# Attention scores on 64 rows of TensorE, two heads in turn, and begun ahead of the value projection

## The chip, the cores and the metric

One core of one Trainium2 chip runs the whole program in one launch. The metric is the device time in microseconds (us), the median over timed runs of the same program on the same chip; lower is better. The profile is of one more execution, and its own time stands beside its span below.

## What is computed

The reference is a decoder trunk of two layers on 256 tokens of width 1024, in float32. Layer 0 mixes tokens with a gated recurrence, layer 1 with sparse attention; each is followed by an MLP with squared ReLU. The change lies in layer 1, the attention. There are 16 query heads of 64 columns in 4 groups of 4, and each group has keys and values of its own in three branches: compressed (15 blocks), selected and sliding window. With 256 tokens, at most 4 blocks to select from and a window of 512, the selected and the window branch both see all earlier tokens; they differ in keys and values. Cut to what matters here:

```python
s_c = jnp.einsum('qghd,ngd->ghqn', qf, kc) - slopes * d_c      # compressed keys
s_s = jnp.einsum('qghd,gqkd->ghqk', qf, k_sel) - slopes * d_s  # selected keys
s_w = jnp.einsum('qghd,kgd->ghqk', qf, kw) - slopes * d_w      # window keys
p_c, p_s, p_w = (_masked_softmax(s, m) for s, m in ((s_c, m_c), (s_s, m_s), (s_w, m_w)))
o = g[..., 0:1] * (p_c @ v_c) + g[..., 1:2] * (p_s @ v_s) + g[..., 2:3] * (p_w @ v_w)
```

## The kernel before

**Split numbers.** Large products are done with numbers split in two: hi is the float32 value rounded to the float32r type, lo is what the rounding left. A product of weights and activations is three matmuls that add up in one PSUM bank (`mm3`, lines 317 to 320): hi x hi, hi x lo, lo x hi. A weight piece (128 x 1024 numbers, 512 KB) is loaded by SP into one of five raw buffers, split by ACT or DVE into `whi` (a cast), and by DVE into `wlo` (a subtraction, `diff`, line 323).

**The planner.** In the attention section nothing is issued directly. Each step is put to a `Plan` with its engine, an estimated duration, what it reads and writes, and a due time `t`. `Plan.emit` makes a list schedule from that and improves it in a few rounds; the order in which each engine issues is the order of the plan's start times. The constants at the top (`TSTAGE`, `FPS`, `SEEDS`) shift due times and choose among plans.

**The attention section** (from line 828) does the following. `cproj` makes the inputs of the compressed branch, `hidden` (L955) and `kc_out` (L965), `vc_out` (L984) its keys and values. `kchunk` projects keys of two groups at once, so that 128 partitions hold 2 groups x 64 columns, and `qchunk` projects queries of two heads at once in the same way. `values` (L1005 to L1007) projects values and gates in four pieces. Then for each of 16 heads `scores` (L1098, L1099) multiplies queries with keys, DVE (L1109, L1116) adds the distances and takes the largest while it copies the rows out of PSUM, ACT (L1112) takes the exponential, `rescale` divides by the sums, `transposes` (L1147) turns the rows, and `pv` (L1162) multiplies with the values, each matmul of it writing 64 of 128 partitions (one head of two). `compressed` (L1072 its transpose) does the compressed branch for four heads. Projections of the later queries and keys and of the output (`out_t`) are laid between as fillers.

**How one score product uses 128 rows.** A head has only 64 columns, and hi and lo of the queries are packed into the two halves of the 128 partitions. For a head in the lower half, the query tile `sa` holds hi in both halves at first, and then its other half is overwritten with lo by a DMA inside the chip (`move`, issued by SP); `sb` does the same for the head in the upper half. The keys `kh` hold hi twice, in both halves (again by a `move`), so that one matmul gives hi x hi + hi x lo; `kl` holds lo in the head's own half and zeros, set by a memset on POOL, in the other, so that a second matmul adds lo x hi:

```python
e.matmul(view(z()), x[:, qs], keys_(kh), start=True, stop=False)   # L1098
e.matmul(view(z()), x[:, qs], keys_(kl), start=False, stop=True)   # L1099
```

Three such parts make a head: the first 128 queries against 128 keys of both branches and the compressed ones (288 columns), the second 128 against 256 keys of one branch and the compressed ones (272), and against 256 of the other (256). Each part takes one of three banks (`sbank`), which is free again when DVE has read it.

Of the kernel before, what the change touches and what calls it, by code (L numbers as in the profile page):

```python
# [19 lines left out]
P = 128  # L20
# [11 lines left out]
NPT, NTL = 3, 3  # L32
TSTAGE, FPS = 5.0, 3.25
CST = (3.5, 7.5, 11.5, 15.2)
SEEDS, ROUNDS, SHIFT = (64, 5), 6, 1.5
# [16 lines left out]
def weight_pieces():  # L52

    order = []
    order += [{"c": ("in", 8 + i), "y": ("in", i)}[k] for k, i in RG_ORDER if k != "g"]
    order += [("out", m) for m in range(8)]
    order += mlp_pieces(0)
    order += [("ck", 0), ("ck", 1), ("cv", 0), ("cv", 1), ("ks", 0), ("kw", 0)]
    order += [("v", i) for i in range(4)]
    order += [("q", m) for m in range(4)]  # L60
    order += [("ks", 1), ("kw", 1)]
    order += [("q", m) for m in range(4, 8)]
    order += [("o0", m) for m in range(4)]
    order += [("o1", m) for m in range(4)]
    order += mlp_pieces(1)
    return order
# [153 lines left out]
def trunk_kernel(ctx: ExitStack, tc: tile.TileContext, x_in, vec_in, const_in, w2_in, wts, out):  # L220
# [607 lines left out]
    with ExitStack() as ph:  # L828
# [12 lines left out]
        tt, tl = many([P, S], F32, "tt", 3), many([P, S], F32R, "tl", NTL)  # L841
# [4 lines left out]
        kh, kl = (at.tile([P, 4 * GK + NCP], F32R, name=n) for n in ("kh", "kl"))  # L846
        kpair = lambda y, g, n: y[:, g * GK:g * GK + 2 * (S + NCP)].rearrange("p (b k) -> p b k", b=2)[:, :, :n]
        kcomp = lambda y: y[:, :4 * GK].rearrange("p (g k) -> p g k", g=4)[:, :, P:PC]
# [20 lines left out]
        add("pool", 1.74, lambda e: e.memset(kl.bitcast(F32), 0.0), w=["kl"], t=-9)  # L869
# [3 lines left out]
        def turn():  # L873
            ti["n"] += 1
            n = ti["n"]
            return tt[n % 3], ("tt", n % 3), tl[n % NTL], ("tl", n % NTL)
# [6 lines left out]
        def qchunk(c, b, t, step):  # L883
            z, zk = proj_t("q", c, b, t, step)
            t += 4 * step
            x, xk, l_, lk = turn()
            a, b_ = sa[c % NQ], sb[c % NQ]
            ak, bk = ("sa", c % NQ), ("sb", c % NQ)
            add("dve", 0.4, lambda e: e.scalar_tensor_tensor(x, z(), cst[:, C_QS + c:C_QS + c + 1], rs,
                                                             op0=OP.mult, op1=OP.mult), r=[zk, "rs"], w=[xk], t=t)  # L890
            add(HI, copy(a, x), r=[xk], w=[ak, ak + (1,)], t=t + 0.5)
            add(HI, copy(b_, x), r=[xk], w=[bk, bk + (1,)], t=t + 0.5)
            add("dve", 0.34, diff(l_, x, a), r=[xk, ak, ak + (1,)], w=[lk], t=t + 1)
            move(a[64:], l_[:64], [lk], [ak + (1,)], t + 1.2)
            move(b_[:64], l_[64:], [lk], [bk + (1,)], t + 1.2)

        def kchunk(gp, br, b, t, step):
            z, zk = proj_t(("ks", "kw")[br], gp, b, t, step)
            t += 4 * step
            x, xk, l_, lk = turn()  # L900
            add("dve", 0.34, lambda e: e.tensor_tensor(x, z(), rs, op=OP.mult), r=[zk, "rs"], w=[xk], t=t)
            x, l_ = two_blocks(x), two_blocks(l_)
            for hf in range(2):
                g = gp * 2 + hf
                add(HI, copy(kset(kh, g, br), x), r=[xk], w=[("k", g, br), ("k", g, br, 1)], t=t + 0.5)
            add("dve", 0.34, diff(l_, x, kset(kh, gp * 2, br)), r=[xk, ("k", gp * 2, br), ("k", gp * 2, br, 1)], w=[lk], t=t + 1)
            for hf in range(2):
# [4 lines left out]
        def kkeys(g, br):  # L912
            return [("k", g, br), ("k", g, br, 1), ("k", g, br, 2)]
# [20 lines left out]
        def cproj(i, gp, b, t, step):  # L934
            z, zk = proj_t(("ck", "cv")[i], gp, b, t, step)
            t += 4 * step
            x, xk, _, _ = turn()
# [25 lines left out]
        def kc_out(t):  # L963
# [4 lines left out]
            add("act", 0.1, lambda e: e.copy(kcomp(kh), o4()), r=[("ps", 6)], w=["kch"], t=t)  # L968
            for hf in range(2):
                own = own_(hf)  # L970
                add("dve", 0.15, lambda e, own=own, hf=hf: e.tensor_tensor(
                    kcomp(kl)[own, hf::2], o4()[own, hf::2], kcomp(kh)[own, hf::2].bitcast(F32), op=OP.subtract),
                    r=[("ps", 6), "kch", "kl"], w=[("kcl", hf)], t=t)
# [17 lines left out]
        def values(t):  # L991
            banks = ((2, 3), (4, 5))
            ncol = (S + 48, S)
            vz = [[zview(("v", h, b), banks[h][b], lambda x, b=b: x[:, :ncol[b]]) for b in range(2)] for h in range(2)]
            for i in range(4):
                wh, wl, wk = weight("v", i, t + 2.8 * i)
                for kk in range(2):
                    k = 2 * i + kk
                    for h in range(2):
                        def run(e, wh=wh, wl=wl, k=k, kk=kk, h=h):  # L1000
# [8 lines left out]
                            t=t + 2.8 * i + 1.4 * kk + 0.7 * h)  # L1009
            t += 11.2  # L1010
# [64 lines left out]
        def scores(s, t):  # L1075
            p, c, hf = heads[s]
            g = 2 * p + hf
            slope = float(2.0 ** (-8.0 * (g * 4 + c + 1) / 16))
            cc = (4 * p + c) % NQ
            x, xk = (sb, sa)[1 - hf][cc], ("sb" if hf else "sa", cc)  # L1080
            xk = [xk, xk + (1,)]
            mx, sm, pt = mxs[s % 4], sms[s % 4], pts[s % NPT]
            a, cj = s // 4, s % 4
            cview = lambda y, n, k: y[:, :2 * n].rearrange("p (b k) -> p b k", b=2)[:, :, :k]
            parts = ((0, lambda x: cview(x, PC, PC), lambda y: kpair(y, g, PC), (0, 1), 0.26),
                     (1, lambda x: x[:, :S + NCP], lambda y: y[:, g * GK:g * GK + S + NCP], (0,), 0.25),
                     (1, lambda x: x[:, :S], lambda y: y[:, g * GK + S + NCP:(g + 1) * GK], (1,), 0.23))
            for i, (qc, view, keys_, sets, d) in enumerate(parts):
                nk = (qc + 1) * P
                n = sn["n"]  # L1090
                sn["n"] += 1
                b = sbank[n % 3]
                bk = [("ps", b)]
                z = zview(("s", s, i), b, lambda x: x)

                def run(e, z=z, qc=qc, view=view, keys_=keys_):
                    qs = slice(qc * P, (qc + 1) * P)
                    e.matmul(view(z()), x[:, qs], keys_(kh), start=True, stop=False)  # L1098
                    e.matmul(view(z()), x[:, qs], keys_(kl), start=False, stop=True)  # L1099
                add("pe", d, run, r=xk + ["kl", "kch", ("kcl", 0), ("kcl", 1)] + kkeys(g, 0) + kkeys(g, 1), w=bk, t=t)  # L1100
                for b in sets:
                    o, j = qc * 2 * P + b * nk, 2 * qc + b
                    mk, pk = ("mx", s % 4, j), ("pt", s % NPT, qc, b)
                    row = pt[:, o:o + nk]
                    dist = cst[:, C_D0 + qc * P:C_D0 + qc * P + nk]
                    src = (lambda z, b=b: cview(z(), PC, P)[:, b]) if qc == 0 else (
                        (lambda z: z()[:, :S]) if b else lambda z: cview(z(), PC, P))
                    shape = two_blocks if (qc, b) == (1, 0) else lambda y: y
                    add("dve", (0.2, 0.34)[qc], lambda e, z=z, src=src, shape=shape, dist=dist, row=row, j=j: e.tensor_tensor_reduce(  # L1109
                        shape(row), src(z), shape(dist), -slope, -NEG, OP.add, OP.min, mx[:, j:j + 1]),  # L1110
                        r=bk + ["cst"], w=[mk, pk], t=t + 0.3)
                    add("act", (0.39, 0.49)[qc], lambda e, row=row, j=j: e.activation(  # L1112
                        row, row, AF.Exp, bias=mx[:, j:j + 1], scale=-1.0, accum_out=sm[:, j:j + 1]), r=[mk, "tab"],
                        w=[pk, ("sm", s % 4, j)], t=t + 0.6)
                if 0 in sets:
                    add("dve", 0.22, lambda e, z=z, qc=qc: e.tensor_tensor_reduce(  # L1116
                        css[a % 2][:, cj, qc], z()[:, P:PC], cst[:, C_DC + qc * NCP:C_DC + (qc + 1) * NCP], -slope, -NEG, OP.add,
                        OP.min, cmx[a % 2][:, 2 * cj + qc:2 * cj + qc + 1]),
                        r=bk + ["cst", ("sq", 0), ("sq", 1)], w=[("cs", a % 2), ("cm", a % 2)], t=t + 0.35)
# [96 lines left out]
        fillers = [("q", c) for c in (1, 2, 3)] + [("ks", 1), ("kw", 1)] + [("q", c) for c in (4, 5, 6, 7)]  # L1216
        step = T / FPS
        events = []
        for i, (nm, c) in enumerate(fillers):
            t = T0 + 4 * i * step  # L1220
# [4 lines left out]
        for m in range(8):  # L1225
            t = T0 + (n0 + 2 * m) * step
# [171 lines left out]
```

## Time and profile before

| | |
|---|---|
| median of 3 runs | 570.66 us (570.56 to 570.67) |
| the profiled execution's own time | 571.1 us |
| its span, first to last instruction | 569.3 us |
| mean granted TensorE clock | 0.996 |
| busy share: TensorE, DVE, ACT, POOL | 99%, 71%, 60%, 7% |
| attention section, from its first projections to the sums of its last normalization (L426) | about 264 to 394 us of the span |
| score products (L1098, L1099) | 305.4 to 367.8 us |

In the views quoted below, PE is TensorE's matmuls, PEld its loads of weights (the stationary operand, which each matmul has), DVE VectorE, ACT ScalarE, POOL GpSimd, SP the queue that issues most DMAs. L1098 is line 1098 of the kernel. A row of the order of time has the start and the duration in us, engine, line, operation, output<-inputs, rows x columns of the array after the names (64*128 is 64 rows, 128*64 is 64 columns), and the moving operand. The durations of matmuls are modelled and overlap, so what a matmul takes is read from start to start. A row of the groups ends with busy us, mean ns of one, and the idle time before it with who ended it.

### The profile page before, as it was taken

The page shows a single profiled execution, that of the slowest core. Times are in us where ns is not written, and L with a number is a line of the kernel's source. Part 1 is how long each engine was busy: PE and PEld are TensorE (multiplying, and loading weights), DVE is VectorE, ACT ScalarE, POOL GpSimd, SP SyncE. Part 2 cuts the span into 40 slices and gives each one's busy share as a digit, 9 for nine tenths or more (in the row PEclk, how much of TensorE's full clock was granted, in tenths as well). Part 3 has the DMA queues.
Part 4 walks back from the last instruction along what each step waited for, and adds up shares of the span by engine and source line. Part 5 has one row for each costly group of instructions (what it writes and reads, how often), then busy time and mean ns, then how long its engine had stood idle before and what let it go on. Part 6 is the DMA issues. An engine that isn't in the chain of part 4 may idle for free.

```text
span 569.3 us, 12420 instructions
## 1 busy us (share of the span) xinstructions
PE 560.9 (99%) x4906; PEld 553.7 (97%) x4906; DVE 407.0 (71%) x877; ACT 342.7 (60%) x666; POOL 40.1 (7%) x55
## 2 busy tenths in 40 slices
PE   9999999999999999999999999999999999999995
PEld 8989999999999999999999999999999999999995
DVE  6999989766775664565749999989867775553532
ACT  7799675865664443444456988886865664443410
POOL 1000000000000211221000000000000000222310
PEclk9999999999999999999999999999999999999998
DMA  8936468556657456456685232354676666566402
GB/s 318 407 98 209 121 214 255 184 189 191 195 194 235 155 204 222 163 190 221 212 264 154 65 114 57 112 171 144 198 230 193 191 202 231 156 205 218 126 1 74
DMA packets 33225, 103.66 MB, mean 182 GB/s; under 512 B 3856, under 2 KB 8080, under 8 KB 33168
## 3 DMA queue, kind: packets, MB, share of 16 engines
q1 hardware_dynamic: 32624, 102.42, 55.8%
q8 instruction: 38, 0.62, 0.4%
q10 hardware_dynamic: 544, 0.46, 0.2%
q14 instruction: 19, 0.16, 0.1%
HBM read 99.23 MB, written 1.05 MB: 176 GB/s over the span
## 4 chain that ended last, share of the span: by engine, by line
PE 95%; DVE 2%; issue 1%; DMA 1%; ACT 1%; DVEq 0%; POOL 0%; SPq 0%; ACTq 0%; POOLq 0%
PE bank L318 28%; PE bank L319 27%; PE bank L320 27%; PE bank L1162 3%; PE bank L686 2%; PE bank L1147 2%; PE bank L1098 1%; PE bank L1099 1%; PE bank L567 1%; DMA pt<-tt 1%; PE bank L1005 1%; DVE wlo L323 1%; PE bank L1006 1%; PE bank L1007 1%; ACT whi L326 1%
## 5 line engine op out<-in xcount | busy, mean ns | idle before, releaser
L318 PE MATMUL bank<-hhl,whi 128*128 128x256 f32 x768 | 213.2, 278 | 0.0
L319 PE MATMUL bank<-hhl,whi 128*128 128x256 f32 x768 | 212.4, 277 | 0.0
L320 PE MATMUL bank<-hhl,wlo 128*128 128x256 f32 x768 | 212.2, 276 | 0.0
L287 DVE TENSOR_TENSOR wlo<-raw,whi 128x1024 fp32r<-128x1024 f32 x115 | 143.2, 1266 | 1.9 <-ACT whi L278 1.9
L319 PEld LDWEIGHTS bank<-hhl,whi 128*128 128x128 f32 x768 | 144.3, 188 | 0.3 <-DVE hhl L576 0.2
L318 PEld LDWEIGHTS bank<-hhl,whi 128*128 128x128 f32 x768 | 144.3, 188 | 0.1
L320 PEld LDWEIGHTS bank<-hhl,wlo 128*128 128x128 f32 x768 | 144.2, 188 | 0.0
L318 PE MATMUL bank<-uhl,whi 128*128 128x256 f32 x512 | 141.5, 276 | 0.0
L319 PE MATMUL bank<-uhl,whi 128*128 128x256 f32 x512 | 141.4, 276 | 0.0
L320 PE MATMUL bank<-uhl,wlo 128*128 128x256 f32 x512 | 141.4, 276 | 0.0
L278 ACT CAST whi<-raw 128x1024 fp32r<-128x1024 f32 x116 | 118.1, 1039 | 23.1 <-issue 18.8
L318 PEld LDWEIGHTS bank<-uhl,whi 128*128 128x128 f32 x512 | 96.1, 188 | 0.0
L319 PEld LDWEIGHTS bank<-uhl,whi 128*128 128x128 f32 x512 | 96.1, 188 | 0.0
L320 PEld LDWEIGHTS bank<-uhl,wlo 128*128 128x128 f32 x512 | 96.1, 188 | 0.0
L323 DVE TENSOR_TENSOR wlo<-raw,whi 128x1024 fp32r<-128x1024 f32 (+2 forms) x72 | 77.4, 1091 | 7.0 <-ACT whi L326 6.9
L326 ACT CAST whi<-raw 128x1024 fp32r<-128x1024 f32 (+2 forms) x63 | 60.0, 966 | 21.4 <-PE bank L319 9.1
L522 DVE TENSOR_TENSOR xt<-xt,bank 128x256 f32<-128x256 f32 x39 | 15.9, 418 | 75.8 <-PE bank L320 75.8
L783 ACT ACTIVATE u<-t 128x256 f32<-128x256 f32 x64 | 26.7, 418 | 58.8 <-DVE t L778 58.6
L778 DVE SCALAR_TENSOR_TENSOR t<-bank,rstd 128x256 f32<-128x256 f32 x64 | 26.9, 423 | 39.7 <-PE bank L320 39.5
L1112 ACT ACTIVATE pt<-pt,mx 128x256 f32<-128x256 f32 (+1 forms) x64 | 28.7, 450 | 3.6 <-DVE mx L1109 3.2
L785 DVE TENSOR_TENSOR uhl<-u,uhl 128x256 fp32r<-128x256 f32 x64 | 26.6, 416 | 3.0 <-ACT uhl L784 3.0
L498 ACT ACTIVATE hhl<-xt,vec 128x256 fp32r<-128x256 f32 x8 | 4.1, 510 | 39.4 <-DVE xt L522 39.4
(201 smaller groups left out, 730.5 us busy)
## 6 DMA issues: line engine op xcount, KB each, us to landing
raw<-in_dram SPq DMA_DIRECT2D x171, 512.0 KB, 4.4
raw<-in_dram SPq DMA_DIRECT2D x4, 560.0 KB, 4.7
gw<-in_dram SPq DMA_DIRECT2D x4, 512.0 KB, 8.3
raw<-in_dram SPq DMA_DIRECT2D x6, 256.0 KB, 5.2
y<-in_dram SPq DMA_DIRECT2D x2, 512.0 KB, 6.8
pT<-in_dram SPq DMA_DIRECT2D x2, 512.0 KB, 5.7
xt<-in_dram SPq DMA_DIRECT2D x3, 256.0 KB, 5.2
kh<-kh SPq DMA_DIRECT2D x8, 64.0 KB, 2.8
```

Of the source, the lines that this page charges most:

```text
L278: (act.copy if eng is None else eng.tensor_copy)(hi_t[i % NSPL][:, :n], raw_of(i)[:, :n])
L287: (eng or dve).tensor_tensor(lo[:, :n], raw_of(i)[:, :n], hi[:, :n].bitcast(F32), op=OP.subtract)
L318: pe.matmul(ps, wh, xh, start=start, stop=False)
L319: pe.matmul(ps, wh, xl, start=False, stop=False)
L320: pe.matmul(ps, wl, xh, start=False, stop=stop)
L323: return lambda e: e.tensor_tensor(o, a, h.bitcast(F32), op=OP.subtract)
L326: return lambda e: (e.copy if e is act else e.tensor_copy)(o, a)
L778: dve.scalar_tensor_tensor(t, z, 0.0, rs, op0=OP.max, op1=OP.mult)
L783: act.activation(u, t, AF.Square)
L785: later(lambda: dve.tensor_tensor(ul[m], u, uh[m].bitcast(F32), op=OP.subtract))
L1112: add("act", (0.39, 0.49)[qc], lambda e, row=row, j=j: e.activation(row, row, AF.Exp, bias=mx[:, j:j + 1], scale=-1.0, accum_out=sm[:, j:j ...
L1162: two = lambda c, w, y, **k: [e.matmul(o()[own_(hf), c0 + c.start:c0 + c.stop], w(hf), y(hf), **k) for hf in range(2)]
```

## The change

- **Scores on 64 rows.** Queries and keys are no longer packed. `sa` holds hi of two heads (64 partitions each), `sb` their lo; `kh` and `kl` hold hi and lo of the keys of two groups, and are half as wide. A score is three matmuls of 64 rows, hi x hi, lo x hi and hi x lo of keys and queries, and the two heads of a pair alternate: one uses rows 0 to 63 of the array, the other rows 64 to 127, each with a bank of its own.
- **No copies.** One copy of each query chunk and one of each key chunk go, so do all moves of queries and keys and the memset of `kl`. The `tl` buffers go. The copy of the compressed keys becomes two, one for each half.
- **Order.** A first query piece comes ahead of the values in the order of weights, and a second one in the midst of them. `values` is put in two halves, in banks 4 to 7, and the first scores are due ahead of them; the first two pairs of heads use two of the score banks, later pairs three. There are six `pt` buffers for three, and the constants of the planner differ.

The core of the diff:

```diff
-NPT, NTL = 3, 3
-TSTAGE, FPS = 5.0, 3.25
+NPT = 6
+TSTAGE, FPS = 5.0, 3.5
+V0, T1 = 20.5, 5.0
-    order += [("v", i) for i in range(4)]
-    order += [("q", m) for m in range(4)]
+    order += [("q", 0), ("v", 0), ("v", 1), ("q", 1), ("v", 2), ("v", 3), ("q", 2), ("q", 3)]
...
-        add("pool", 1.74, lambda e: e.memset(kl.bitcast(F32), 0.0), w=["kl"], t=-9)
...
-            a, b_ = sa[c % NQ], sb[c % NQ]
-            ak, bk = ("sa", c % NQ), ("sb", c % NQ)
+            h, l_, hk, lk = sa[c % NQ], sb[c % NQ], ("sa", c % NQ), ("sb", c % NQ)
...
-            add(HI, copy(a, x), r=[xk], w=[ak, ak + (1,)], t=t + 0.5)
-            add(HI, copy(b_, x), r=[xk], w=[bk, bk + (1,)], t=t + 0.5)
-            add("dve", 0.34, diff(l_, x, a), r=[xk, ak, ak + (1,)], w=[lk], t=t + 1)
-            move(a[64:], l_[:64], [lk], [ak + (1,)], t + 1.2)
-            move(b_[:64], l_[64:], [lk], [bk + (1,)], t + 1.2)
+            add(HI, copy(h, x), r=[xk], w=[hk], t=t + 0.5)
+            add("dve", 0.34, diff(l_, x, h), r=[xk, hk], w=[lk], t=t + 1)
...
-            for hf in range(2):
-                own, oth, g = own_(hf), own_(1 - hf), gp * 2 + hf
-                move(kset(kh, g, br)[oth], kset(kh, g, br)[own], [("k", g, br)], [("k", g, br, 1)], t + 0.8)
-                move(kset(kl, g, br)[own], l_[own], [lk, "kl"], [("k", g, br, 2)], t + 1.2)
+            h, l_, x2_ = kset(kh, gp, br), kset(kl, gp, br), two_blocks(x)
+            add(HI, copy(h, x2_), r=[xk], w=[("kh", gp, br)], t=t + 0.5)
+            add("dve", 0.34, diff(l_, x2_, h), r=[xk, ("kh", gp, br)], w=[("kl", gp, br)], t=t + 1)
...
-                def run(e, z=z, qc=qc, view=view, keys_=keys_):
+                bs = [sbank[(sn["n"] + hf) % (3 if sp > 1 else 2)] for hf in range(2)]
+                sn["n"] += 2
+                zs = [zview(("s", 2 * sp + hf, i), bs[hf], lambda x: x) for hf in range(2)]
+
+                def run(e, zs=zs, qc=qc, view=view, keys_=keys_):
                     qs = slice(qc * P, (qc + 1) * P)
-                    e.matmul(view(z()), x[:, qs], keys_(kh), start=True, stop=False)
-                    e.matmul(view(z()), x[:, qs], keys_(kl), start=False, stop=True)
+                    for n, (k, y) in enumerate(((kh, xh), (kh, xl), (kl, xh))):
+                        for hf in range(2):
+                            own = own_(hf)
+                            e.matmul(view(zs[hf]()), y[own, qs], keys_(k, p)[own], start=n == 0, stop=n == 2)
+                add("pe", d, run, r=xk, w=[("ps", b) for b in bs], t=t)
+                for hf, z in enumerate(zs):
+                    taken(2 * sp + hf, z, [("ps", bs[hf])], qc, nk, sets, t)
...
-        table(AF.Exp, 24)
-        values(20.5)
-        gate_t(34)
-        qchunk(0, 6, 34, PJ)
-        T0, T = 37.0, TSTAGE
+        table(AF.Exp, 22)
+        qchunk(0, 0, V0, PJ)
+        values(0, V0 + 2.7)
+        qchunk(1, 1, V0 + 8.3, PJ)
+        values(1, V0 + 11)
+        gate_t(V0 + 17)
+        T0, T, F0 = V0 + T1, TSTAGE, V0 + 17.0
...
         for s in range(16):
-            events.append((T0 + s * T, 1, lambda s=s: scores(s, T0 + s * T)))
+            if s % 2 == 0:
+                events.append((T0 + s * T, 1, lambda s=s: scores(s // 2, T0 + s * T)))
```

`taken` holds what stood in `scores` behind the matmuls (the reads by DVE, the exponential by ACT), word for word but for the tiles. In the changed kernel the score matmuls are L1085, the transposes L1142 and L1061, the values L992 to L994, the products with the values L1157, and the compressed branch L941, L951 and L971.

More of the change, by code (lines that the diff above doesn't have):

```diff
@@ L845, in trunk_kernel @@
         GK, PC = 2 * S + NCP, P + NCP
[L846 removed]
+        kh, kl = (at.tile([P, i * GK + NCP], F32R, name=n) for n, i in (("kh", 2), ("kl", 2)))
         kpair = lambda y, g, n: y[:, g * GK:g * GK + 2 * (S + NCP)].rearrange("p (b k) -> p b k", b=2)[:, :, :n]
[L848 removed]
+        kcomp = lambda y: y[:, :2 * GK].rearrange("p (g k) -> p g k", g=2)[:, :, P:PC]
         def kset(y, g, br):
@@ L936, in cproj @@
             t += 4 * step
-            x, xk, _, _ = turn()
+            x, xk = turn()
             add("dve", 0.34, lambda e: e.tensor_tensor(x, z(), rs, op=OP.mult), r=[zk, "rs"], w=[xk], t=t)
@@ L989, in vc_out, with values @@
                     cst[:, C_BM:C_BM + 8, None].to_broadcast([P, 8, 64]), op=OP.mult), r=[("ps", 7)], w=[("bd", p)], t=t)
-        def values(t):
-            banks = ((2, 3), (4, 5))
+        def values(part, t):
+            banks = ((4, 5), (6, 7))
             ncol = (S + 48, S)
             vz = [[zview(("v", h, b), banks[h][b], lambda x, b=b: x[:, :ncol[b]]) for b in range(2)] for h in range(2)]
-            for i in range(4):
-                wh, wl, wk = weight("v", i, t + 2.8 * i)
+            for j, i in enumerate((2 * part, 2 * part + 1)):
+                wh, wl, wk = weight("v", i, t + 2.8 * j)
                 for kk in range(2):
@@ L1008, in values @@
                         add("pe", 0.7, run, r=wk + [hkey[k]], w=[("ps", banks[h][0]), ("ps", banks[h][1])],
-                            t=t + 2.8 * i + 1.4 * kk + 0.7 * h)
-            t += 11.2
+                            t=t + 2.8 * j + 1.4 * kk + 0.7 * h)
+            if part == 0:
+                return
+            t += 5.6
             for h in range(2):
@@ L1073, in compressed, with scores @@
             add([("act", 0.3, 0.0), ("dve", 0.2, 0.15)], lambda e: copy(pc, ct_())(e), r=b7, w=[pk], t=t)
[L1075 to L1078, printed above, removed]
+        def scores(sp, t):
+            p, c, _ = heads[2 * sp]
             cc = (4 * p + c) % NQ
[L1080 to L1083, printed above, removed]
+            xh, xl = sa[cc], sb[cc]
+            xk = [("sa", cc), ("sb", cc)] + [(n, hf) for n in ("kch", "kcl") for hf in range(2)]
+            xk += [(n, p, br) for n in ("kh", "kl") for br in range(2)]
@@ L1100, in scores @@
[L1100 to L1114, printed above, removed]
@@ new lines, in scores, with taken @@
+                add("pe", d, run, r=xk, w=[("ps", b) for b in bs], t=t)
+                for hf, z in enumerate(zs):
+                    taken(2 * sp + hf, z, [("ps", bs[hf])], qc, nk, sets, t)
+        def taken(s, z, bk, qc, nk, sets, t):
+            p, c, hf = heads[s]
+            slope = float(2.0 ** (-8.0 * ((2 * p + hf) * 4 + c + 1) / 16))
+            a, cj = s // 4, s % 4
+            mx, sm, pt = mxs[s % 4], sms[s % 4], pts[s % NPT]
+            cview = lambda y, n, k: y[:, :2 * n].rearrange("p (b k) -> p b k", b=2)[:, :, :k]
+            for b in sets:
+                o, j = qc * 2 * P + b * nk, 2 * qc + b
+                mk, pk = ("mx", s % 4, j), ("pt", s % NPT, qc, b)
+                row = pt[:, o:o + nk]
+                dist = cst[:, C_D0 + qc * P:C_D0 + qc * P + nk]
+                src = (lambda z, b=b: cview(z(), PC, P)[:, b]) if qc == 0 else (
+                    (lambda z: z()[:, :S]) if b else lambda z: cview(z(), PC, P))
+                shape = two_blocks if (qc, b) == (1, 0) else lambda y: y
+                add("dve", (0.2, 0.34)[qc], lambda e, src=src, shape=shape, dist=dist, row=row, j=j: e.tensor_tensor_reduce(
+                    shape(row), src(z), shape(dist), -slope, -NEG, OP.add, OP.min, mx[:, j:j + 1]),
+                    r=bk + ["cst"], w=[mk, pk], t=t + 0.3)
+                add("act", (0.39, 0.49)[qc], lambda e, row=row, j=j: e.activation(
+                    row, row, AF.Exp, bias=mx[:, j:j + 1], scale=-1.0, accum_out=sm[:, j:j + 1]), r=[mk, "tab"],
+                    w=[pk, ("sm", s % 4, j)], t=t + 0.6)
+            if 0 in sets:
+                add("dve", 0.22, lambda e: e.tensor_tensor_reduce(
+                    css[a % 2][:, cj, qc], z()[:, P:PC], cst[:, C_DC + qc * NCP:C_DC + (qc + 1) * NCP], -slope, -NEG, OP.add,
+                    OP.min, cmx[a % 2][:, 2 * cj + qc:2 * cj + qc + 1]),
+                    r=bk + ["cst", ("sq", 0), ("sq", 1)], w=[("cs", a % 2), ("cm", a % 2)], t=t + 0.35)
```

46 lines of the change are left out of this document (15 added, 31 removed).

## The prediction

> **What bounds the kernel now.** I read the page first, then who made TensorE wait, then the attention stage by stretches, then the order of time around the score products. The page says that one engine is the kernel:
>
> ```profile
> span 569.3 us, 12420 instructions
> PE 560.9 (99%) x4906; PEld 553.7 (97%) x4906; DVE 407.0 (71%) x877; ACT 342.7 (60%) x666; POOL 40.1 (7%) x55
> ...
> PE 95%; DVE 2%; issue 1%; DMA 1%; ACT 1%; DVEq 0%; POOL 0%; SPq 0%; ACTq 0%; POOLq 0%
> ```
>
> A busy share of 99% proves little by itself, since the ends of matmuls are modelled. The list of TensorE's waits bears it out: in 569 us it waited for others five times, and these are the three that matter here (us in total, times, longest).
>
> ```profile
> PE bank L567 <- POOL warm L562: 1.3, 1, 1.3
> PE bank L955 <- DMA pt<-tt: 0.4, 1, 0.4
> PE bank L965 <- ACT sq L959: 0.4, 1, 0.4
> ```
>
> The first is the start of the program. The other two stand at the compressed keys, at the beginning of the attention section. Between 305 and 375 us, where the change works, TensorE waited for nobody:
>
> ```profile
> 285.00:290.00 5.00, 4.66 (x34) 4.47 (x35) 2.69 (x7) 3.42 (x7) 0.00 (x0) 1.00 0.95 349
> 305.00:375.00 70.00, 70.00 (x656) 66.89 (x656) 66.39 (x347) 61.44 (x199) 0.00 (x0) 1.00 0.29 89
> ```
>
> The columns are us, PE, PEld, DVE, ACT and POOL busy, the granted clock (1.00) and the share of the DMA engines. DVE is at 66.39 of 70 us, so it is the next limit, but TensorE sets the time. The question is thus how much time of TensorE the new score products take, and nearly all else is cover.
>
> **What a score product costs now.** One head, in order of time (start, modelled duration):
>
> ```profile
> 305.45 0.29 PE L1098 MATMUL bank<-kh,sa 128*128 128x272 f32 x1
> 305.57 0.29 PE L1099 MATMUL bank<-kl,sa 128*128 128x272 f32 x1
> 305.70 0.30 PE L1098 MATMUL bank<-kh,sa 128*128 128x288 f32 x1
> 305.84 0.30 PE L1099 MATMUL bank<-kl,sa 128*128 128x288 f32 x1
> 305.97 0.28 PE L1098 MATMUL bank<-kh,sa 128*128 128x256 f32 x1
> 306.09 0.28 PE L1099 MATMUL bank<-kl,sa 128*128 128x256 f32 x1
> 306.21 0.28 PE L318 MATMUL bank<-hhl,whi 128*128 128x256 f32 x1
> ```
>
> What counts is start to start: 0.125 us for 272 columns, 0.135 for 288, 0.12 for 256, and 0.76 for the head; 16 heads take 12.2 us. Nothing is lost at the edges: the projection follows at once.
>
> The change puts three products of 64 rows for each head in place of two of 128, 144 matmuls for 96, two heads in turn on different row groups. If the two of a turn run side by side, a pair of heads has three turns of each length: 3 x (0.125 + 0.135 + 0.12) = 1.14 us, and eight pairs take 9.1. **First term: -3.0 us.** Whether they do is not shown for row groups, but it is for column groups, where the products with the values write 64 partitions each:
>
> ```profile
> 29.63 12.95 PE bank L686 x60
> 324.35 3.62 PE bank L1162 x48
> L686 PE MATMUL bank<-xb,gw x64: 378/379/380, 29.5 to 43.8; 128*128 128x256 f32 x64
> L1162 PE MATMUL bank<-pT,vv x128: 272/326/379, 324.8 to 377.9; 128*64 128x256 f32 x64, 128*64 128x128 f32 x64
> ```
>
> A plain f32 matmul of 256 columns takes 12.95 / 60 = 0.216 us. A burst of L1162 has 16 with 256 columns and 32 with 128, one after the other 6.9 us; it took 3.62. So halves of the array do work at once.
>
> **What the edges cost: the term that decides.** Each time the array goes from whole to halves or back, the starts show a hole. Into column halves, out of them, and out of row halves (L984, 64 rows):
>
> ```profile
> 323.96 0.28 PE L319 MATMUL bank<-hhl,whi 128*128 128x256 f32 x1
> 324.07 0.28 PE L320 MATMUL bank<-hhl,wlo 128*128 128x256 f32 x1
> 324.28 0.55 PE L1162 MATMUL bank<-pc,bd 128*64 128x128 f32 x6
> ```
> ```profile
> 360.37 0.27 PE L1162 MATMUL bank<-pT,vv 128*64 128x128 f32 x1
> 360.57 0.39 PE L318 MATMUL bank<-oh,whi 128*128 128x256 f32 x1
> 360.79 0.28 PE L319 MATMUL bank<-ol,whi 128*128 128x256 f32 x1
> ```
> ```profile
> 286.14 0.27 PE L984 MATMUL bank<-w2raw,sq 64*128 64x64 f32 x1
> 286.35 0.41 PE L1005 MATMUL bank<-whi,hhl 128*128 128x304 f32 x1
> 286.59 0.30 PE L1006 MATMUL bank<-wlo,hhl 128*128 128x304 f32 x1
> 286.73 0.30 PE L1007 MATMUL bank<-whi,hhl 128*128 128x304 f32 x1
> ```
>
> Into halves: 0.21 from start to start where 0.11 is the pace, so 0.10 lost, and then the first load of weights stands bare. Out of column halves: 0.20 (0.10 lost), then 0.22 before the second matmul where 0.11 is the pace (0.11 lost for the bare load). Out of row halves: 0.21 against 0.11, then 0.24 against 0.14, again 0.20 in all. So one change of the array's shape costs 0.20 us, and rows cost what columns do. The way into row halves is in no row of before. The Trainium skill has a rule on it that speaks against this change: TensorEngine Tiling (Array Packing), section Key Properties, says that a change of tiling mode, unlike a change of tile within one mode, drains TensorE. By it the way in costs like the way out; the three edges above agree, and it gives no figure of its own.
>
> How many changes come is read from TensorE's order. Before, at the first scores (kh, kl are keys, sa holds queries, hhl and whi a projection):
>
> ```order
> L320 MATMUL bank_3726<-hhl,wlo_92 128x256
> L1098 MATMUL bank_3760<-kh,sa_3225 128x272
> L1099 MATMUL bank_3760<-kl,sa_3225 128x272
> L1098 MATMUL bank_3766<-kh,sa_3225 128x288
> L1099 MATMUL bank_3766<-kl,sa_3225 128x288
> L1098 MATMUL bank_3769<-kh,sa_3225 128x256
> L1099 MATMUL bank_3769<-kl,sa_3225 128x256
> L318 MATMUL bank_3773<-hhl,whi_86 128x256
> ```
>
> Six products of one shape in a row, in the shape of their neighbours. Now, at the first scores, which lie among the value projection (L992 to L994, whole array):
>
> ```order
> L994 MATMUL bank_3591<-whi_87,hhl 128x256
> L1085 MATMUL bank_3602<-kh,sa_3225 128x288
> L1085 MATMUL bank_3604<-kh,sa_3225 128x288
> L1085 MATMUL bank_3602<-kh,sb_3229 128x288
> L1085 MATMUL bank_3604<-kh,sb_3229 128x288
> L1085 MATMUL bank_3602<-kl,sa_3225 128x288
> L1085 MATMUL bank_3604<-kl,sa_3225 128x288
> L992 MATMUL bank_3587<-whi_88,hhl 128x304
> ```
>
> One part of two heads, and then the whole array again. And late in the section, with transposes (L1142, L1061) between:
>
> ```order
> L1142 MATMUL bank_4543<-cst,pt 128x128 x3
> L1085 MATMUL bank_4551<-kh,sa_3227 128x272
> L1085 MATMUL bank_4553<-kh,sa_3227 128x272
> L1085 MATMUL bank_4551<-kh,sb_3231 128x272
> L1085 MATMUL bank_4553<-kh,sb_3231 128x272
> L1085 MATMUL bank_4551<-kl,sa_3227 128x272
> L1085 MATMUL bank_4553<-kl,sa_3227 128x272
> L1061 MATMUL bank_4562<-cst,sq_112 128x128
> L1142 MATMUL bank_4566<-cst,pt 128x128 x3
> L1142 MATMUL bank_4570<-cst,pt 128x128 x3
> L1085 MATMUL bank_4578<-kh,sa_3227 128x256
> ```
>
> All 24 parts stand alone like this: none has another part beside it, and only four of their 48 edges touch products with the values, which are halves already. The whole program changes shape 14 times before and 58 times now. **Second term: 44 x 0.20 = +8.8 us.** For the 24 ways into row halves the lower end is zero (-4.8 us; below that nothing can go, since 0.11 from start to start is the floor everywhere); the upper end, if the two first loads come one after the other, is a load more, which rival 3 puts at 0.11: +2.6. I take 0.20, because the way out of rows cost what the way out of columns did.
>
> **What is hidden.** The copies and moves that go (one of two copies of each query and key chunk, 32 DMAs inside the chip, two for each of 8 query and four for each of 4 key chunks, a memset of kl):
>
> ```profile
> L326 DVE CAST sb<-tt 128x256 fp32r<-128x256 f32 x7 | 2.0, 288 | 0.0
> L326 ACT CAST kh<-tt 128x256 fp32r<-128x256 f32 x5 | 2.0, 413 | 2.8 <-DVE tt L901 2.8
> kh<-kh SPq DMA_DIRECT2D x8, 64.0 KB, 2.8
> sa<-tl SPq DMA_DIRECT2D x8, 64.0 KB, 1.9
> ```
>
> They free some 4 us of DVE and ACT (12 copies at 0.29 to 0.41) and SP's queue, where weight loads stood behind them. TensorE waited for none of it, so I count nothing; were DVE the limit, it would be worth up to those 4 us. The order of weights changes (one query piece ahead of the values) in the stretch 285 to 290 us, where DMA is 0.95 busy; TensorE had no wait for weights there and the bytes are the same, so zero again. Scores that start earlier spread DVE's work over more time; no gain while TensorE sets the pace. **Third term: -0.8 us:** in the new order twelve more projection matmuls come ahead of the hidden layer of the compression (L955) and twelve stand between it and L965, 1.3 us each time at 0.11, more than the two waits of 0.4, so both go.
>
> **Sum.** +8.8 - 3.0 - 0.8 = +5.0 us. The profiled execution took 571.1 us (span 569.3), which would become 576.1; the median of the runs, 570.66, is 0.44 lower: **575.7**. With half of the ways in gone (-2.4) or a load more at each (+2.6) this case spans 573.3 to 578.3. Chance 0.62.
>
> **Rivals.** (1) *The way into row halves is nearly free*, 570.9 to 573.3, and half of that lies within 0.2% of before (1.1 us, about what a measurement tells from no change). For: no row shows it. Against: the way into columns cost 0.10 before any load. Chance 0.10.
>
> (2) *Faster: row groups change without a hole.* If the hole at L1005 belonged to that place (a wait, its first use of a bank) and not to the change of shape, only the gains stay, -3.8 us: **566.9**. It decides below 3.8 / 44 = 0.09 us a change. Against: the same two gaps at column edges. Chance 0.10.
>
> (3) *The two heads don't run side by side*, since their weight loads come in series. Loads for 64 rows:
>
> ```profile
> 285.76 0.52 PEld L984 LDWEIGHTS bank<-w2raw,sq 64*128 64x128 f32 x4
> 286.34 0.19 PEld L1005 LDWEIGHTS bank<-whi,hhl 128*128 128x128 f32 x1
> ```
>
> Four in 0.52 with the last at 0.19: one each 0.11. In series a turn is 0.22, not 0.127: 72 x 0.095 = +6.8 on the sum, **582.5**; with the products in series too, 72 more of 0.127, 584.8. For: column halves load only 64 columns each, so their pairs don't test it. Against: two groups of rows share nothing that a trace shows. Chance 0.05. In another form a load waits for the product of its own group; a turn is then 0.11 + 0.127, 72 x 0.11 = +7.9, 583.6. Against: whole-array matmuls of before stand 0.11 apart while each load lasts 0.19. Chance 0.02. The Trainium skill, TensorE: Matmul & The Clock Gate, Part 3, states that form as a rule (a load overlaps running matmuls only where the row group differs); the trace of before disagrees with it.
>
> (4) *New waits for banks.* A part now takes two of three banks at once, and the next can't start until DVE has read the first:
>
> ```profile
> L1109 DVE CUSTOM_DVE_ANT_0 pt<-bank,cst 128x256 f32<-128x256 f32 x32 | 13.2, 418 | 1.0 <-PE bank L1099 0.9
> L1109 DVE CUSTOM_DVE_ANT_0 pt<-bank,cst 128x128 f32<-128x128 f32 x32 | 8.7, 285 | 0.6 <-PE bank L1099 0.6
> L323 DVE TENSOR_TENSOR wlo<-raw,whi 128x1024 fp32r<-128x1024 f32 x28 | 33.8, 1218 | 6.9 <-ACT whi L326 6.9
> ```
>
> Where six transposes (0.66) stand between two parts, a read of 0.42 fits, but not behind a weight split of 1.22. Ten gaps are under 1.9 us; a wait at four of them, about one split each, is +3 to +5: 578.7 to 580.7, since all that is queued behind on TensorE waits too. Against: TensorE gets 5 us longer and DVE 4 us less to do. Chance 0.11.
>
> Range 571.5 to 581.0: it leaves out (2), (3) and the lower part of (1). Faster 0.10, same 0.05, slower 0.85.
>
> **What would show it.** Right: each L1085 group starts about 0.2 after the matmul ahead and the matmul behind shows a longer first gap; starts within a group come in pairs, with 0.12 to 0.135 from pair to pair; TensorE's waits stay under 2 us. Wrong: gaps at the edges of 0.11 to 0.13 (2); pairs 0.22 apart (3); L1085 waiting for DVE by several us (4).

## The result and the profile after

| | before | after |
|---|---|---|
| median, same chip | 570.66 us (569.71 to 570.96, 5 runs) | 575.56 us (574.74 to 576.1, 5 runs) |
| ratio of after to before | | 1.0086, 95% interval 1.0071 to 1.0101 |
| the profiled execution's own time | 571.1 us | 574.98 us |
| its span | 569.3 us | 573.2 us |
| granted TensorE clock | 0.996 | 0.998 |

The change costs 4.9 us; the prediction was 5.0. The page of the changed kernel: the span, the busy time of the engines, and the chain that ended last by engine.

```profile
span 573.2 us, 12426 instructions
PE 565.5 (99%) x4954; PEld 552.0 (96%) x4954; DVE 405.9 (71%) x868; ACT 341.9 (60%) x664; POOL 38.3 (7%) x54
...
PE 99%; DVE 0%; DVEq 0%; ACT 0%; POOL 0%; issue 0%; POOLq 0%
```

There are 48 matmuls more (144 score products for 96), and the chain is TensorE's for 99% where it was 95%: the kernel got slower while TensorE waited less. The list of all its waits (us in total, times, longest):

```profile
PE bank L567 <- POOL warm L562: 1.3, 1, 1.3
PE bank L1266 <- ACT sqh L1264: 0.4, 1, 0.4
PE bank L1272 <- DVE rc L1271: 0.3, 1, 0.3
```

Both waits at the compressed keys are gone, and no wait at a score product has come. So no wait holds the lost time; it lies between matmuls that waited for nobody. Here is the first visit to the row halves, in order of time (x2 is one product of each head):

```profile
290.58 0.28 PE L994 MATMUL bank<-whi,hhl 128*128 128x256 f32 x1
290.79 0.41 PE L1085 MATMUL bank<-kh,sa 64*128 64x288 f32 x2
291.03 0.30 PE L1085 MATMUL bank<-kh,sb 64*128 64x288 f32 x2
291.16 0.30 PE L1085 MATMUL bank<-kl,sa 64*128 64x288 f32 x2
291.39 0.41 PE L992 MATMUL bank<-whi,hhl 128*128 128x304 f32 x1
291.63 0.30 PE L993 MATMUL bank<-wlo,hhl 128*128 128x304 f32 x1
291.77 0.30 PE L994 MATMUL bank<-whi,hhl 128*128 128x304 f32 x1
```

Read it from start to start. The pace of the matmuls ahead is 0.12 (256 columns, as before). Into row halves 0.21 pass, and 0.24 more to the second turn, where a turn of 288 columns takes 0.13 (the next step). Out of them 0.23, and 0.24 to the second matmul, where its pace is 0.14. The excess is (0.21 - 0.12) + (0.24 - 0.13) = 0.20 for the way in and (0.23 - 0.13) + (0.24 - 0.14) = 0.20 for the way out. Each part of the scores pays this twice.

Four edges join scores and the products with the values, two each way. One from row halves to column halves:

```profile
342.05 0.28 PE L1085 MATMUL bank<-kh,sb 64*128 64x256 f32 x2
342.17 0.28 PE L1085 MATMUL bank<-kl,sa 64*128 64x256 f32 x2
342.38 0.66 PE L1157 MATMUL bank<-pc,bd 128*64 128x128 f32 x8
```

The way from rows into columns takes 0.21 (342.17 to 342.38) where 0.12 is the pace, and then 0.16 to the second pair of products (merged in the row) where 0.11 is; the kernel before has the same two times from the whole array into columns at 324.07 us. The way back, columns to rows, takes 0.20 and then 0.24. Halves beside other halves do not save the edge.

Last, DVE's reads of the scores, both forms in one group (busy, mean ns of one, idle before them and who ended it):

```profile
L1104 DVE CUSTOM_DVE_ANT_0 pt<-bank,cst 128x128 f32<-128x128 f32 (+1 forms) x64 | 20.8, 354 | 9.2 <-PE bank L1085 8.9
```

DVE now waits 9.2 us for scores, where it waited 1.0 + 0.6 before: it has moved further from being the limit, which speaks against rival 4.

### The profile page after: what moved, and what is told of

It is laid out like the page before. It is cut to its first block, busy times and chain, and to the rows that moved or that the text cites. A ratio compares the mean times of both kernels' runs of the same rounds, so it can differ in the third digit from the quotient of the medians.

```text
span 573.2 us, 12426 instructions
## 1 busy us (share of the span) xinstructions
PE 565.5 (99%) x4954; PEld 552.0 (96%) x4954; DVE 405.9 (71%) x868; ACT 341.9 (60%) x664; POOL 38.3 (7%) x54
## 3 DMA queue, kind: packets, MB, share of 16 engines
HBM read 99.23 MB, written 1.05 MB: 175 GB/s over the span
## 4 chain that ended last, share of the span: by engine, by line
PE 99%; DVE 0%; DVEq 0%; ACT 0%; POOL 0%; issue 0%; POOLq 0%
PE bank L318 29%; PE bank L319 28%; PE bank L320 28%; PE bank L1157 3%; PE bank L686 2%; PE bank L1085 2%; PE bank L1142 2%; PE bank L992 1%; PE bank L567 1%; PE bank L993 1%; PE bank L994 1%; PE bank L941 1%; DVE xg L1280 0%; PE bank L1061 0%; PE bank L519 0%; PE bank L514 0%
## 5 line engine op out<-in xcount | busy, mean ns | idle before, releaser
L320 PE MATMUL bank<-hhl,wlo 128*128 128x256 f32 x768 | 212.4, 277 | 0.0
L320 PEld LDWEIGHTS bank<-hhl,wlo 128*128 128x128 f32 x768 | 144.2, 188 | 0.2 <-DVE wlo L323 0.2
L320 PE MATMUL bank<-uhl,wlo 128*128 128x256 f32 x512 | 141.4, 276 | 0.0
L320 PEld LDWEIGHTS bank<-uhl,wlo 128*128 128x128 f32 x512 | 96.1, 188 | 0.0
L326 ACT CAST whi<-raw 128x1024 fp32r<-128x1024 f32 (+2 forms) x64 | 61.1, 968 | 16.2 <-PE bank L319 5.4
```

The costliest lines, as they stand in the source:

```text
L320: pe.matmul(ps, wl, xh, start=False, stop=stop)
L326: return lambda e: (e.copy if e is act else e.tensor_copy)(o, a)
```

## The experiments

The theory is that of the prediction: less time in the products, +0.20 for each change of the array's shape, and all else hidden. Its rivals were an edge that costs something else than a change of shape, heads that do not run side by side, and costs or gains in what was counted at zero. Medians stand beside runs of the kernel before on the same chip (570.69 us for e1 to e4, 570.80 for e5 to e8, 570.84 for e9 to e11).

**e1, the changed kernel without row halves.** Each turn is one product of 128 rows, in the same place.

```diff
                     for n, (k, y) in enumerate(((kh, xh), (kh, xl), (kl, xh))):
-                        for hf in range(2):
-                            own = own_(hf)
-                            e.matmul(view(zs[hf]()), y[own, qs], keys_(k, p)[own], start=n == 0, stop=n == 2)
+                        e.matmul(view(zs[n // 2]()), y[:, qs], keys_(k, p), start=n != 1, stop=n > 0)
```

> The changed kernel with each turn of two 64-row products made one product of 128 rows on the whole array, so three per part and 72 in all, in the same order and with the same reads behind them. It leaves out that the two heads are kept apart: the scores are sums over both heads, so the output is not the reference's. No score changes the array's shape any more (14 changes in the program for 58). Theory (a change of shape costs 0.20 us, 44 of them): 575.6 - 8.8 = 566.8, with no hole at the edges of a part. Rival (the holes belong to the place, to short visits of six with banks of their own, whatever the shape): about 575, holes as in the changed kernel.

Measured: 567.12 us (566.63 to 568.27), ratio to before 0.9942 (0.9930 to 0.9954). The same scores as above, in order of time:

```profile
291.37 0.28 PE L994 MATMUL bank<-whi,hhl 128*128 128x256 f32 x1
291.48 0.29 PE L1083 MATMUL bank<-kh,sa 128*128 128x288 f32 x1
291.62 0.30 PE L1083 MATMUL bank<-kh,sb 128*128 128x288 f32 x1
291.75 0.29 PE L1083 MATMUL bank<-kl,sa 128*128 128x288 f32 x1
291.88 0.31 PE L992 MATMUL bank<-whi,hhl 128*128 128x304 f32 x1
292.02 0.30 PE L993 MATMUL bank<-wlo,hhl 128*128 128x304 f32 x1
```

No edge: 0.11 to 0.14 throughout. From the last matmul ahead to the second behind this takes 0.65 us (291.37 to 292.02); in the changed kernel 1.05 (290.58 to 291.63). The 44 changes of shape thus cost 575.56 - 567.12 = 8.44 us, 0.192 each; with the intervals of both medians, 0.17 to 0.22. And all the rest of the change is worth 567.12 - 570.69 = -3.6 us: the kernel would have become faster but for the edges.

**e2, one head after the other.** The same products, but all three of one head come first.

```diff
-                    for n, (k, y) in enumerate(((kh, xh), (kh, xl), (kl, xh))):
-                        for hf in range(2):
-                            own = own_(hf)
+                    for hf in range(2):
+                        own = own_(hf)
+                        for n, (k, y) in enumerate(((kh, xh), (kh, xl), (kl, xh))):
```

> The changed kernel with the three products of one head ahead of the three of the other within each part, nothing else moved. Theory (products on different row groups run side by side, those on one group do not): five turns per part in place of three, 24 x 2 x 0.127 = +6.1 us, 581.7; starts 0.12 to 0.135 apart within a head. Rival (the pace within a part has nothing to do with the turn of row groups): 575.6.

Measured: 575.62 us (575.31 to 576.31), ratio 1.0089 (1.0077 to 1.0102): as the changed kernel. The theory's number fell, and the rival's came. The order of time shows why:

```profile
290.78 0.28 PE L994 MATMUL bank<-whi,hhl 128*128 128x256 f32 x1
290.99 0.41 PE L1085 MATMUL bank<-kh,sa 64*128 64x288 f32 x2
291.22 0.31 PE L1085 MATMUL bank<-kh,sb 64*128 64x288 f32 x2
291.36 0.30 PE L1085 MATMUL bank<-kl,sa 64*128 64x288 f32 x2
```

The program has kh,sa, kh,sb, kl,sa of one head and then the same of the other. The trace has both heads' kh,sa together, then both kh,sb. The second head's first product, fourth in the program, stands beside the first one, ahead of the second and third. Turns in the program are not needed for the two heads to overlap.

**e7, both heads on the same rows.** That leaves the question what makes them overlap. Here the second head uses rows 0 to 63 too (its scores are then not the reference's), and all else stays.

```diff
-                            own = own_(hf)
+                            own = own_(0)
```

> The changed kernel with the products of both heads on rows 0 to 63, where the second head uses the first one's queries and keys (its scores are wrong for that); the same changes of shape. After the order within a part made no difference, this tells whether the two heads run side by side because they are on different rows. Theory: six in a row in place of three turns, 24 x 3 x 0.127 = +9.1, 584.7. Rival (64-row products overlap anyway): 575.6.

Measured: 584.03 us (583.56 to 584.68), ratio 1.0234 (1.0220 to 1.0248).

```profile
295.87 0.52 PE L1085 MATMUL bank<-kh,sa 64*128 64x272 f32 x2
296.23 0.41 PE L1085 MATMUL bank<-kh,sb 64*128 64x272 f32 x2
296.48 0.41 PE L1085 MATMUL bank<-kl,sa 64*128 64x272 f32 x2
296.83 0.41 PE L992 MATMUL bank<-whi,hhl 128*128 128x304 f32 x1
```

From the second turn to the third 0.25 now pass where 0.13 did: two products of one row group go one after the other. Over 24 parts of three turns, 584.03 - 575.56 = 8.5 us is 0.118 for each turn, one product more. So the overlap in the changed kernel comes from the two row groups, and it halves the time of a turn.

**e5 and e6, the price of a change by itself.** Both add 18 matmuls without use to the projections of the kernel before, ahead of or behind whole runs of products. In e5 they use the whole array, in e6 only rows 0 to 63; the edit is otherwise the same.

```diff
+                    visit = lambda: e.matmul(full()[:, S:], wh[:, :P], xs[0][0], start=True, stop=True)          # e5
+                    visit = lambda: e.matmul(full()[:, S:], wh[:64, :P], xs[0][0][:64], start=True, stop=True)   # e6
+                    if len(ks) == 4 and ks[0] == 0:
+                        visit()
                     for k in ks:
                         w = slice(k * P, (k + 1) * P)
                         mm3(z(), wh[:, w], wl[:, w], xs[k][0], xs[k][1], k == 0, k == KC - 1)
+                    if len(ks) == 4 and ks[0] == 4:
+                        visit()
```

> The kernel before with 18 extra matmuls in the attention section, one ahead of and one behind each of the nine projections there: whole array, 256 columns, into columns of the projection's bank that nobody reads, 14 changes of shape as before. Every theory: 18 x 0.113 = +2.0 us, 572.7. It is the control of the next one.

> As the control, but each of the 18 extra matmuls takes rows 0 to 63 alone; 47 changes of shape for 14, no other edit and the same order. Theory (a change costs 0.20 us wherever it stands): control + 33 x 0.20 = +6.6, 579.3. Rival (the holes of the changed kernel belong to its score parts, their banks or their pairs): as the control, 572.7.

Measured: 572.42 us (571.3 to 573.78) for e5, ratio 1.0034 (1.0020 to 1.0049); 578.75 us (578.13 to 580.68) for e6, ratio 1.0146 (1.0128 to 1.0165). One such matmul (L398) in each, e5 first:

```profile
305.17 0.28 PE L320 MATMUL bank<-hhl,wlo 128*128 128x256 f32 x1
305.28 0.28 PE L398 MATMUL bank<-hhl,whi 128*128 128x256 f32 x1
305.40 0.29 PE L1104 MATMUL bank<-kh,sa 128*128 128x272 f32 x1
305.52 0.29 PE L1105 MATMUL bank<-kl,sa 128*128 128x272 f32 x1
```
```profile
305.27 0.28 PE L320 MATMUL bank<-hhl,wlo 128*128 128x256 f32 x1
305.48 0.38 PE L398 MATMUL bank<-hhl,whi 64*128 64x256 f32 x1
305.79 0.39 PE L1104 MATMUL bank<-kh,sa 128*128 128x272 f32 x1
306.02 0.29 PE L1105 MATMUL bank<-kl,sa 128*128 128x272 f32 x1
```

0.35 us from L320 to the second product behind in the one, 0.75 in the other: 0.40 for two changes. Over the program 578.75 - 572.42 = 6.33 us for 47 - 14 = 33 changes, again 0.192 each (0.15 to 0.23 with the intervals, so that the third digit agrees by luck). The price belongs to the change of shape and to no operation, tile or place of the score products. Rival 2 is out.

**e3 and e4, the two parts of the change apart.** e3 has the packed scores of before with the new order of weights and the new due times (the first two query pieces around the values, the values in two halves, the first scores due ahead of them); e4 has the 64-row scores, without copies and moves, in the order of before. The core of e3:

```diff
-    order += [("v", i) for i in range(4)]
-    order += [("q", m) for m in range(4)]
+    order += [("q", 0), ("v", 0), ("v", 1), ("q", 1), ("v", 2), ("v", 3), ("q", 2), ("q", 3)]
...
-        values(20.5)
-        gate_t(34)
-        qchunk(0, 6, 34, PJ)
+        qchunk(0, 0, V0, PJ)
+        values(0, V0 + 2.7)
+        qchunk(1, 1, V0 + 8.3, PJ)
+        values(1, V0 + 11)
+        gate_t(V0 + 17)
```

and of e4 (the rest as in the diff of the change):

```diff
-                    e.matmul(view(z()), x[:, qs], keys_(kh), start=True, stop=False)
-                    e.matmul(view(z()), x[:, qs], keys_(kl), start=False, stop=True)
+                    for n, (k, y) in enumerate(((kh, xh), (kh, xl), (kl, xh))):
+                        for hf in range(2):
+                            own = own_(hf)
+                            e.matmul(view(zs[hf]()), y[own, qs], keys_(k, p)[own], start=n == 0, stop=n == 2)
```

> The kernel before with its packed 128-row scores, copies and moves, but with the new order: query pieces among the values, the values in two halves on banks 4 to 7, the first scores due ahead of them. Theory (the order only takes away the two waits of 0.4 us): 569.9, within 0.3% of before; 14 changes of shape. Rival (the order itself costs, because DVE or the moves get late): over 572, with TensorE's waits at the scores. Rival (the early scores are worth more, and the rows took more than 8.8 - 3.0): under 569.

> The changed kernel's 64-row scores without copies and moves, in the order of before (values in one go, scores behind them). 60 changes of shape for 14. Theory: 570.7 + 46 x 0.20 - 3.0 = 576.9, the two waits at the compression still there. Rival (the order carries the loss): about 568 to 571.

Measured: e3 573.81 us (572.64 to 574.61), ratio 1.0055 (1.0040 to 1.0069), a clear miss; e4 577.65 us (576.45 to 579.78), ratio 1.0123 (1.0103 to 1.0142), 0.75 above the number expected. TensorE's waits in the attention section, e3 and then e4:

```profile
PE bank L955 <- DMA pt<-tt: 1.0, 1, 1.0
PE bank L1149 <- ACT pt L1138: 0.9, 2, 0.7
```
```profile
PE bank L971 <- DVE sq L326: 0.5, 1, 0.5
PE bank L941 <- DMA pt<-tt: 0.5, 1, 0.5
...
PE bank L1140 <- ACT pT L326: 0.3, 1, 0.3
...
PE bank L1140 <- DVE pT L326: 0.3, 1, 0.3
```

Before, the two waits at the compression are 0.4 + 0.4. In e3 one of them is 1.0, and transposes (L1149) wait 0.9 for ACT's part of `rescale` (L1138). In e4 (L941 is the hidden layer, L971 the compressed values) they are 0.5 + 0.5, and transposes wait 0.6. The changed kernel has none of these. That accounts for e4: it has 0.8 of waits more than before and came 0.75 above the number expected; and it is 577.65 - 575.56 = 2.1 us above the changed kernel, of which the waits are 1.6 and two more changes of shape 0.4.

e3 is not the changed kernel's order with packed scores, though. From the new due times the planner made another order: the first twelve query products stand behind the hidden layer, where the changed kernel has them ahead of it, and the first scores come at 295.6 us, where the changed kernel has them at 290.8. e3 also keeps three `pt` buffers and the planner's seeds of before. In its profiled execution (574.52 us, 3.4 more than that of before), 0.7 of the 3.4 has passed ahead of the hidden layer, where both programs are the same; score products and transposes take 2.2 more from start to start (0.9 of it in the waits above), the hidden layer 0.7 more and the projections 0.5 more, the values 0.6 less.

**e8, fewer visits.** For the last six pairs of heads, the second and third part go together, with bank 7 as a fourth bank: 48 changes of shape in place of 58.

```diff
+                if i == 2 and sp > 1:
+                    bs = [sbank[sn["n"] % 3], 7]
+                    sn["n"] += 1
...
+                    def both(e, run=run, zs1=zs1, qc1=qc1, view1=view1, keys1=keys1):
+                        run(e, zs1, qc1, view1, keys1)
+                        run(e)
+                    add("pe", 0.73, both, r=xk, w=[("ps", b) for b in bs1 + bs], t=t)
```

> The changed kernel with the second and third part of a pair of heads in one stretch of twelve products, for the last six pairs, with bank 7 as the fourth bank; 48 changes of shape for 58. Theory: 575.6 - 10 x 0.20 = 573.6. Rival (the place decides, or the larger stretches wait for banks): 575 to 577, with TensorE waiting for DVE at the scores.

Measured: 576.22 us (575.08 to 576.93), ratio 1.0093 (1.0079 to 1.0107): no gain on the changed kernel, whose ratio is 1.0086 (1.0071 to 1.0101).

```profile
PE bank L1174 <- DVE ol L323: 0.9, 1, 0.9
...
PE bank L1159 <- ACT pT L326: 0.4, 1, 0.4
PE bank L1061 <- DVE sq L1049: 0.3, 1, 0.3
```

Ten changes less should give 1.9 us; three waits that the changed kernel does not have take 1.6. None of them is at a score product, as rival 4 had it. The longest is at the products with the values (L1174): their last two bursts both write bank 7 and follow each other in e8, so the second waits until DVE has read the first; the changed kernel has six projection products between the two (379.21 to 380.22 us) and no wait. So the fewer changes came with a plan that waits elsewhere; that four banks at once are the cause is not shown.

**e9, the moves left out.**

```diff
-            move(a[64:], l_[:64], [lk], [ak + (1,)], t + 1.2)
-            move(b_[:64], l_[64:], [lk], [bk + (1,)], t + 1.2)
+            idle(a[64:], l_[:64], [lk], [ak + (1,)], t + 1.2)
+            idle(b_[:64], l_[64:], [lk], [bk + (1,)], t + 1.2)
...
-                move(kset(kh, g, br)[oth], kset(kh, g, br)[own], [("k", g, br)], [("k", g, br, 1)], t + 0.8)
-                move(kset(kl, g, br)[own], l_[own], [lk, "kl"], [("k", g, br, 2)], t + 1.2)
+                idle(kset(kh, g, br)[oth], kset(kh, g, br)[own], [("k", g, br)], [("k", g, br, 1)], t + 0.8)
+                idle(kset(kl, g, br)[own], l_[own], [lk, "kl"], [("k", g, br, 2)], t + 1.2)
```

> The kernel before, with its 32 DMA moves of queries and keys left out and nothing else: the plan keeps a place for each, so the order stays that of before (the score products then read halves that don't hold the packed numbers, so the output is not the reference's). It prices the term that was counted at zero. Theory (the moves are hidden, TensorE waits for none of them): as before, 570.7 us, within 0.5. Rival (SP's queue behind the moves, or the moves' traffic, holds up weights that TensorE needs): 569.7 or less.

Measured: 570.40 us (569.8 to 571.95), ratio 0.9996 (0.9986 to 1.0007), or by the ratio -0.2 us with an interval from -0.8 to +0.4. The 32 moves cost nothing that can be measured.

**e10 and e11, the kernel before without its two waits.** Both keep the packed scores and the 14 changes of shape and try to fill the 0.4 + 0.4. e10 puts the first query piece ahead of the values, e11 gives the compressed keys a later due time and issues the hidden layer's 64 matmuls as one step (beyond what its expectation says).

```diff
-    order += [("v", i) for i in range(4)]
-    order += [("q", m) for m in range(4)]
+    order += [("q", 0)] + [("v", i) for i in range(4)]
+    order += [("q", m) for m in range(1, 4)]
...
-        values(20.5)
-        gate_t(34)
-        qchunk(0, 6, 34, PJ)
+        qchunk(0, 0, 20.5, PJ)
+        values(23.2)
+        gate_t(36)
```
```diff
-            for q_ in range(4):
+            for q_ in range(1):
...
-        hidden(4, 16)
-        kc_out(20)
-        vc_out(20.5)
+        hidden(4, 17)
+        kc_out(22)
+        vc_out(22)
```

> The kernel before, with packed scores, moves and its 14 changes of shape, and one thing of the change: the first query piece comes ahead of the values in the order of weights and its projection ahead of the compression's second half, so that TensorE has whole-array work where it waited 0.4 twice (L955, L965). Theory (both waits are filled and nothing else moves): 0.4 to 0.8 below before, 569.9 to 570.3. Rival (a new order makes waits of its own, as in e3): 571.5 or more.

> The kernel before, with the compressed keys (L965) due later in the plan, so that products of the value projection stand between L955 and L965, and nothing else. Theory: the wait of 0.4 at L965 goes, the one at L955 stays, 570.3. Rival: the wait comes back at what now stands behind (L971, L984 or the first scores), 570.7 or more.

Measured: e10 572.20 us (571.37 to 573.5), ratio 1.0022 (1.0012 to 1.0033); e11 571.29 us (570.72 to 572.53), ratio 1.0013 (1.0002 to 1.0024). Neither number of the theory came. e10 is slower than before; e11 lies at the edge of the noise, and no gain. The waits, e10 and then e11 (whose profiled execution took 570.72 us, the least of its 12 runs):

```profile
PE bank L955 <- ACT kh L326: 1.4, 1, 1.4
...
PE bank L1098 <- DVE mx L1109: 0.4, 1, 0.4
...
PE bank L965 <- ACT sq L959: 0.3, 1, 0.3
```
```profile
PE bank L320 <- DVE wlo L323: 0.3, 1, 0.3
PE bank L1005 <- ACT sq L959: 0.2, 1, 0.2
PE bank L1147 <- ACT pT L326: 0.2, 1, 0.2
```

In e10 the wait at L955 has grown to 1.4 and now ends with a cast of keys (L326), L965 still waits 0.3, and a score product waits 0.4: 1.3 more than before in all, about what e10 lost. Here too the planner put the first twelve query products behind the hidden layer (L955), so nothing more than before stands ahead of it. In e11 both waits are gone and three smaller ones, 0.7 together, stand elsewhere. No version here beats the kernel before with the reference's scores; e1 is faster, but it sums two heads.

## Why the prediction was right

- **First term, -3.0 (score products).** Right. Within a visit a turn takes 0.12 to 0.13 with both heads in it, as assumed from the column halves, and e7 shows that the row groups are the reason. Together with the third term the prediction had -3.8; e1 measures -3.6 for everything but the edges, and does not part the two.
- **Second term, +8.8 (44 changes of shape).** Right, and it decides the sign: 8.44 us by e1 (0.192 each), 0.192 each by e6, 0.20 in and 0.20 out by the trace. The open point was the way into row halves; it costs what the way out does, so rival 1 (0 for it) is out. The Trainium skill's rule on it (TensorEngine Tiling (Array Packing), Key Properties: a change of mode drains TensorE) agrees with the holes in these traces, 0.192 us a change. One reading beside it was wrong: 0.11 from start to start is no floor everywhere, since the 64 products of the hidden layer stand 0.057 apart (3.62 us in the changed kernel).
- **Third term, -0.8 (two waits go).** The waits went, but one half of the reason was misread and the size is partly luck. The twelve query products ahead of the hidden layer came in all five kernels with the changed order (the changed one, e1, e2, e7, e8), and in each the hidden layer runs through in 3.62 us, where before it took 4.31. e3 and e10 don't speak against it, since their plans put nothing more ahead of L955; no run has the twelve there with packed scores. The twelve between L955 and L965, however, are no addition: before already has twelve products of the values in that place (283.16 to 285.34 us) and waits 0.4, and e10, with twelve of the query instead, still waits 0.3. Why that wait is gone in the changed kernel stays open. Nor is the size firm: e9, e5 and e6 have the order of before up to there, and in their profiled executions the hidden layer waits 0.7, 0 and 0 where before waited 0.4.
- **Hidden work at zero.** Right for the moves (e9, by itself). The copies and the memset were not priced by themselves; DVE's idle time ahead of the score reads rose from 1.6 to 9.2 us, which fits that DVE is not the limit. The order beyond the two waits was counted at zero too, and no run prices it alone: e3 costs 3.1 us, but with a plan of its own.
- **The sum.** +5.0 predicted, +4.9 measured, with an interval from 4.1 to 5.8. The parts by e1, -3.6 and +8.44, add up to the measured change by the way they are made; the check from outside is e6, whose price makes 44 x 0.192 = 8.4 as well. That the sum came within 0.1 is luck: the edges came 0.4 cheaper than forecast, the gain 0.2 smaller.
- **Rivals.** 1 and 2 fell with e6 and the trace, 3 with the pace of the turns in the changed kernel (0.12 to 0.13 us, where its two forms gave 0.22 and 0.24). e7 makes its case of loads and products in series: 584.03 us, where the prediction gave 584.8. 4 did not come: among TensorE's waits none is at a score product, in the changed kernel or in e8.

## What to carry to other kernels

Before splitting a matmul over halves of the array, count the changes of shape that TensorE's order will have, and price each by a hole that the trace already shows: here 0.19 us, two for each visit, so that a visit has to save 0.4 us before it gains, and these saved 0.15 at most (e1's 3.6 us over 24 visits). Fewer changes pay only if the plan that comes with them doesn't wait elsewhere (e8). And where a planner makes the order, look at what it made before you reason from what you asked of it: in e3 and e10 the products that were to fill a gap came behind it.

## What was not expected of the hardware

- TensorE started matmuls out of the order of the program where they use different row groups (e2): the fourth started beside the first, ahead of the second and third, and the time was that of alternating heads (575.62 us beside 575.56). The Trainium skill, TensorE: Matmul & The Clock Gate, Part 3, states that matmuls start and end strictly in the order of the program; in the trace of e2 the starts differ (290.99 us for the fourth, 291.22 for the second).
- A change from row halves to column halves costs like one from the whole array to column halves (0.21 us from start to start where 0.12 is the pace, then 0.16 where 0.11 is, in both), though both are halves.
